# An im2col kernel on one core: four equal stores of two channels, and copies of several planes in one instruction

## The chip, the cores and the metric

The kernel runs on one core of a Trainium2 chip. The metric is the time of one execution on the device in microseconds (us), as a median of several executions. The profile shows one execution by itself; its span, from the first to the last instruction, is about 1.8 us shorter than the time.

"Engine" stands for two things here. VectorE and ScalarE copy data, and SyncE issues the transfers. The transfers themselves are carried by sixteen DMA engines: the page gives the time of the queue's packets as a share of sixteen engines' span, and packets start in rounds of sixteen (in the kernel before, 786 GB/s times 0.50 us are sixteen rows of 24,576 bytes). The views used here do not name a packet's engine. That each engine goes on with its own next packet is read from the times: in the kernel before, the sixteen last load packets end between 11.20 and 11.63 us, and the store's first sixteen packets start at just those times, one for one within 0.02 us. A packet is mostly one row, the bytes of one partition: 24,576 in the second load, 32,400 in a store of one channel, 64,800 in a store of two (112 of the 1008 packets of the kernel before are under 512 bytes). A transfer is *issued* when SyncE hands it to the queue, and has *landed* when its completion is seen.

## The reference

The operation is called im2col (image to columns). The input `x` is 16 images of 64 channels of 32 x 32 float32. For each channel and each of the nine positions (ki, kj) of a 3 x 3 window, the output holds one *plane*: the 30 x 30 elements of the channel that start at (ki, kj).

```python
for i in range(h_out):            # 30
    for j in range(w_out):        # 30
        patch = x[b, :, i:i + kernel_size, j:j + kernel_size].copy()
        cols[b, :, col_idx] = patch.ravel()
        col_idx += 1
```

Nothing is computed. 4.19 MB are read and 33.18 MB are written.

## The kernel before

The 1024 (image, channel) pairs are laid out as 128 partitions of 8 channels. Two loads bring them in: channels 0 and 1 first, then the other six. VectorE and ScalarE copy planes, 900 elements at a time, into an output tile of two channels, of which there are two buffers, and SyncE stores the tile. Channels 0 and 1 are stored separately; the other three pairs have one store each. All transfers go through one DMA queue.

```python
out_pool = ctx.enter_context(tc.tile_pool(name="out_pool", bufs=2))
# ... (cut)
first = load(nc.sync, 0, 2 * H)
load(nc.sync, 2 * H, CPP * H)

on_act = (False, True, False, True, False)
n = 0
for c in range(0, CPP, 2):
    out_tile = out_pool.tile([P, 2, KK, HO, WO], x.dtype, name="out_tile")
    for s in range(2):
        for kk in range(KK):
            ki, kj = divmod(kk, K)
            src = in_tile[:, c + s, ki : ki + HO, kj : kj + WO]
            dst = out_tile[:, s, kk]
            if kk % 3 != 1 if c + s == 0 else on_act[n % len(on_act)]:
                nc.scalar.copy(out=dst, in_=src)
            else:
                nc.vector.tensor_copy(out=dst, in_=src)
            n += 1
        if c == 0:
            nc.sync.dma_start(out=out_v[:, s], ...)           # one channel, arguments cut
    if c > 0:
        nc.sync.dma_start(out=out_v[:, c : c + 2] ..., ...)   # two channels, arguments cut
```

## Time and profile before

| | before |
|---|---|
| time, median of 3 runs | 91.28 us (91.22 to 91.31) |
| span in the profile | 89.5 us |
| VectorE, ScalarE busy | 25%, 31% |
| queue's packets, of sixteen engines' span | 97.2% |
| first store issued | 9.92 us |
| last store issued, landed | 56.64 us, 88.7 us |

The row to start from is the queue's 97.2%: the copying engines idle for most of the span, the transfers hardly ever do.

(A line of a timeline gives start and duration in us, the engine, the line of the kernel, the operation, output<-input and the count; SPq is SyncE issuing transfers.)

### The profile page before, as it was taken

The page shows a single profiled execution, that of the slowest core. Times are in us where ns is not written, and L with a number is a line of the kernel's source. Part 1 is how long each engine was busy: PE and PEld are TensorE (multiplying, and loading weights), DVE is VectorE, ACT ScalarE, POOL GpSimd, SP SyncE. Part 2 cuts the span into 40 slices and gives each one's busy share as a digit, 9 for nine tenths or more (in the row PEclk, how much of TensorE's full clock was granted, in tenths as well). Part 3 has the DMA queues.
Part 4 walks back from the last instruction along what each step waited for, and adds up shares of the span by engine and source line. Part 5 has one row for each costly group of instructions (what it writes and reads, how often), then busy time and mean ns, then how long its engine had stood idle before and what let it go on. Part 6 is the DMA issues. An engine that isn't in the chain of part 4 may idle for free.

```text
span 89.5 us, 136 instructions
## 1 busy us (share of the span) xinstructions
DVE 22.4 (25%) x41; ACT 27.7 (31%) x32; POOL 0.2 (0%) x4
## 2 busy tenths in 40 slices
DVE  0089369900000099400000499200000000000000
ACT  5089999910000099900000499200000000000000
POOL 0000000000000000000000000000000000000000
DMA  5989899999989999996699999999999996779990
GB/s 146 498 373 505 351 463 463 463 463 434 405 376 405 695 463 463 463 405 290 290 405 463 463 463 463 463 463 463 463 463 463 463 463 290 318 318 463 463 463 0
DMA packets 1008, 37.37 MB, mean 417 GB/s; under 512 B 112, under 2 KB 112, under 8 KB 112
## 3 DMA queue, kind: packets, MB, share of 16 engines
q1 hardware_dynamic: 1008, 37.37, 97.2%
HBM read 4.19 MB, written 33.18 MB: 417 GB/s over the span
## 4 chain that ended last, share of the span: by engine, by line
DMA 41%; ACT 15%; DVE 6%; DVEq 1%; issue 0%
DMA out_dram<-out_tile 36%; ACT out_tile L54 15%; DVE out_tile L56 6%; DMA in_tile<-in_x_dram 5%; DVEq L82 1%; DVEq L56 0%
## 5 line engine op out<-in xcount | busy, mean ns | idle before, releaser
L54 ACT COPY out_tile<-in_tile 128x900 f32<-128x900 f32 x31 | 26.5, 938 | 28.0 <-DMA out_dram<-out_tile 25.4
L56 DVE COPY out_tile<-in_tile 128x900 f32<-128x900 f32 x41 | 22.4, 624 | 34.2 <-DMA out_dram<-out_tile 27.1
L54 ACT ACT_TABLE_LOAD x1 | 1.3, 1283 | 0.8 <-PEq L111 0.8
L111 POOL MEMSET const-bfloat16-1.0<- 128x1 bf16 x1 | 0.1, 102 | 0.0
L111 POOL MEMSET const-uint8-127<- 128x1 uint8 x1 | 0.1, 102 | 0.0
L111 POOL MEMSET const-float32-1.0<- 128x1 f32 x1 | 0.1, 99 | 0.0
L111 POOL MEMSET const-float32-0.0<- 128x1 f32 x1 | 0.1, 98 | 0.2 <-issue 0.2
## 6 DMA issues: line engine op xcount, KB each, us to landing
out_dram<-out_tile SPq DMA_DIRECT2D x3, 8100.0 KB, 32.1
out_dram<-out_tile SPq DMA_DIRECT2D x2, 4050.0 KB, 15.3
in_tile<-in_x_dram SPq DMA_DIRECT2D x1, 3072.0 KB, 11.2
in_tile<-in_x_dram SPq DMA_DIRECT2D x1, 1024.0 KB, 4.7
```

Of the source, the lines that this page charges most:

```text
L54: nc.scalar.copy(out=dst, in_=src)
L56: nc.vector.tensor_copy(out=dst, in_=src)
L82: tc.compile()
L111: nc = _bacc.Bacc("TRN2", target_bir_lowering=False, num_devices=1)
```

## The change

The intent is to have fewer and larger instructions and transfers. Planes of one row of the window start one element apart, so one instruction can copy two or three of them if the source pattern gets an additional outermost dimension of step 1. VectorE takes two planes (`kj` 0 and 1) at a time, ScalarE three. In the first channel of each pair VectorE also takes the planes (0, 2) and (2, 2) in one instruction, which start two rows apart; in the second channel these two are copied singly, one by each engine. Channels 0 and 1 are no longer stored apart: there are four equal stores.

```diff
+    def planes(c, ki, kj, n, step):
+        w = in_tile[:, c, ki : ki + HO, kj : kj + WO]
+        part, row, col = [list(d) for d in w.ap]
+        return bass.AP(w.tensor, w.offset, [part, [step, n], row, col])
 ... (cut: the loop over kk, its choice of engine, and the stores of one channel go)
         for s in range(2):
+            o = out_tile[:, s]
+            nc.scalar.copy(out=o[:, K : 2 * K], in_=planes(c + s, 1, 0, K, 1))
+            for ki in (0, 2):
+                nc.vector.tensor_copy(
+                    out=o[:, ki * K : ki * K + 2], in_=planes(c + s, ki, 0, 2, 1)
+                )
+            if s == 0:
+                nc.vector.tensor_copy(
+                    out=o[:, 2:KK:6], in_=planes(c + s, 0, 2, 2, 2 * W)
+                )
+            else:
+                nc.vector.tensor_copy(out=o[:, 2], ...)       # one plane, arguments cut
+                nc.scalar.copy(out=o[:, 8], ...)              # one plane, arguments cut
+        nc.sync.dma_start(out=out_v[:, c : c + 2] ..., ...)   # for every c
```

More of the change, by code (lines that the diff above doesn't have):

```diff
@@ L19, in _im2col @@
     CPP = B * C // P
-    assert CPP * P == B * C and C % CPP == 0 and CPP % 4 == 0
+    assert CPP * P == B * C and C % CPP == 0 and CPP % 2 == 0 and K == 3
     x_v = x.rearrange("b (cp c2) h w -> (b cp) (c2 h w)", c2=CPP)
@@ L31, in _im2col, with load @@
     in_flat = in_tile.rearrange("p c h w -> p (c h w)")
-    def load(queue, r0, r1):
-        return queue.dma_start(
-            out=in_flat[:, r0 * W : r1 * W], in_=x_v[:, r0 * W : r1 * W]
-        )
-    first = load(nc.sync, 0, 2 * H)
-    load(nc.sync, 2 * H, CPP * H)
-    on_act = (False, True, False, True, False)
-    n = 0
+    def load(r0, r1):
+        return nc.sync.dma_start(
+            out=in_flat[:, r0 * W : r1 * W],
+            in_=x_v[:, r0 * W : r1 * W],
+        )
+    first = load(0, 2 * H)
+    load(2 * H, CPP * H)
+    def planes(c, ki, kj, n, step):
+        w = in_tile[:, c, ki : ki + HO, kj : kj + WO]
+        part, row, col = [list(d) for d in w.ap]
+        return bass.AP(w.tensor, w.offset, [part, [step, n], row, col])
     for c in range(0, CPP, 2):
@@ L48, in _im2col @@
         for s in range(2):
-            for kk in range(KK):
-                ki, kj = divmod(kk, K)
-                src = in_tile[:, c + s, ki : ki + HO, kj : kj + WO]
-                dst = out_tile[:, s, kk]
-                if kk % 3 != 1 if c + s == 0 else on_act[n % len(on_act)]:
-                    nc.scalar.copy(out=dst, in_=src)
-                else:
-                    nc.vector.tensor_copy(out=dst, in_=src)
-                n += 1
-            if c == 0:
-                nc.sync.dma_start(
-                    out=out_v[:, s],
-                    in_=out_tile[:, s].rearrange("p kk i j -> p (kk i j)"),
-                )
-        if c > 0:
-            nc.sync.dma_start(
-                out=out_v[:, c : c + 2].rearrange("p c n -> p (c n)"),
-                in_=out_tile.rearrange("p c kk i j -> p (c kk i j)"),
-            )
+            o = out_tile[:, s]
[3 more added lines that the diff above has]
+                    out=o[:, ki * K : ki * K + 2], in_=planes(c + s, ki, 0, 2, 1)
+                )
+            if s == 0:
[3 more added lines that the diff above has]
+            else:
+                nc.vector.tensor_copy(
+                    out=o[:, 2], in_=in_tile[:, c + s, 0:HO, 2 : 2 + WO]
+                )
+                nc.scalar.copy(
+                    out=o[:, 8], in_=in_tile[:, c + s, 2 : 2 + HO, 2 : 2 + WO]
+                )
+        nc.sync.dma_start(
+            out=out_v[:, c : c + 2].rearrange("p c n -> p (c n)"),
+            in_=out_tile.rearrange("p c kk i j -> p (c kk i j)"),
+        )
     return first
```

## The prediction

> **What bounds the kernel now.** I began with the page of the profile. VectorE and ScalarE are busy a quarter and a third of the span; the DMA engines are nearly always busy.
>
> ```profile
> span 89.5 us, 136 instructions
> DVE 22.4 (25%) x41; ACT 27.7 (31%) x32; POOL 0.2 (0%) x4
> q1 hardware_dynamic: 1008, 37.37, 97.2%
> ```
>
> The reader is to see that one DMA queue moves 37.37 MB, and that the time of its packets fills 97.2% of what sixteen engines have. Those bytes (4.19 MB in, 33.18 MB out) are fixed by the task, and the change touches none of them. So what matters is whether the queue ever runs dry. I read the timeline next: when each engine copies, and when each transfer is issued.
>
> ```profile
> 4.74 13.60 ACT L54 COPY out_tile<-in_tile 128x900 f32<-128x900 f32 x16 [2.67 <-DMA in_tile<-in_x_dram]
> 4.74 4.93 DVE L56 COPY out_tile<-in_tile 128x900 f32<-128x900 f32 x9 [4.74 <-DMA in_tile<-in_x_dram]
> 9.92 2.87 SPq L59 DMA_DIRECT2D out_dram<-out_tile  x2
> 12.02 6.00 DVE L56 COPY out_tile<-in_tile 128x900 f32<-128x900 f32 x11 [2.35 <-DMA in_tile<-in_x_dram]
> ...
> 50.56 6.00 DVE L56 COPY out_tile<-in_tile 128x900 f32<-128x900 f32 x11 [13.66 <-DMA out_dram<-out_tile]
> 56.64 0.33 SPq L64 DMA_DIRECT2D out_dram<-out_tile  x1
> ```
>
> The first load lands at 4.7 us, the second at 12.0. The store of channel 0 is issued at 9.92, before the second load has landed. The last store is issued at 56.64 and lands 32.1 us later (DMA issues of the page), at 88.7: it stood in the queue behind others for most of that time. To find gaps in the queue I asked for the table of windows in narrow stretches. Its last two columns are DMA share and GB/s, and a packet is counted in the window in which it starts, so a share can be over 1 and a window without a start shows 0.
>
> ```profile
> 0.00:1.00 1.00, 0.00 (x0) 0.21 (x1) 0.20 (x4) 1.00 0.00 0
> 1.00:1.45 0.45, 0.00 (x0) 0.45 (x1) 0.00 (x0) 1.00 1.43 291
> 10.25:10.75 0.50, 0.00 (x0) 0.50 (x2) 0.00 (x0) 1.00 1.82 786
> 10.75:11.20 0.45, 0.00 (x0) 0.45 (x1) 0.00 (x0) 1.00 0.00 0
> 11.20:11.65 0.45, 0.00 (x0) 0.45 (x2) 0.00 (x0) 1.00 2.69 1152
> 12.35:12.85 0.50, 0.50 (x2) 0.50 (x2) 0.00 (x0) 1.00 2.40 1037
> ...
> 30.35:30.80 0.45, 0.00 (x0) 0.00 (x0) 0.00 (x0) 1.00 5.34 2304
> 32.75:33.20 0.45, 0.45 (x2) 0.45 (x2) 0.00 (x0) 1.00 5.32 2304
> 85.40:85.85 0.45, 0.00 (x0) 0.00 (x0) 0.00 (x0) 1.00 5.33 2304
> ```
>
> Three things are to be seen. First, the sixteen engines start their packets together, spread over about 0.43 us: 786 GB/s times 0.50 us is 393 KB, sixteen rows of 24,576 bytes, the last of the second load; 1152 times 0.45 is 518 KB, sixteen rows of 32,400 bytes, the first of the store. Second, the share gives a packet's time: 1.82 times 0.50 us is 0.91 us. The load's last packets start from about 10.29, so they end from about 11.20, just where the store's first ones start: **no gap**. Third, the rows of the large stores (2304 times 0.45 is 1037 KB, sixteen of 64,800 bytes) take 5.33 times 0.45 = 2.40 us each. From 30.35 to 85.40 lie 55.05 us, which is 23 of them at 2.39. From 11.2 us to the end the queue never waits for the copies: the store of the third buffer is issued at 38.28 and starts at about 49.5, so that compute is over 11 us early.
>
> [...] 16 times 64,800 bytes in 2.39 us is 434 GB/s. [...]
> [...] Here the first load is issued at 0.00 and its first packet starts in the window from 1.00 us on; steps of 0.02 us inside it put the start at about 1.03, and I use this measured value.
> [...] eleven VectorE copies take 6.00 us and one takes 624 ns, so one starts every (6.00 - 0.624)/10 = 538 ns[...]. ScalarE: (13.60 - 0.938)/15 = 844 ns[...].
> [...]
>
> **The change, part by part.**
> (1) Copies are merged. VectorE goes from 41 instructions to 24, ScalarE from 31 copies to 12. One pair of channels costs VectorE five copies of two planes and one of one plane: [...], plus about 0.09 until the last one ends (624 - 538), 5.66. ScalarE has two copies of three planes and one of one: [...], plus 0.09 (938 - 844), 5.63. Before, a pair took 6.00. So 0.34 us is saved for each pair, but for the second, third and fourth pair this lies wholly beside stores that take 19 us each: worth 0.
> (2) The first store is now of two channels, not one. Compute starts at 4.74 as before; the store may be issued at 4.74 + 5.66 + 0.02 = **10.42** in place of 9.92: 0.50 later, although it waits for twice the planes. This is where the merging is needed: at the old cost per plane the 18 planes would have been ready at 4.74 + 6.00 = 10.74.
> (3) What does 0.50 us cost? The engines are free for the store from 11.20. With 1.03 us from issue to first packet, the store starts at 10.42 + 1.03 = 11.45, so the queue would stand still for **0.25 us**. Everything behind it is one chain of packets, so this goes to the end undiminished.
> (4) One transfer less, and no rows of 32,400 bytes: channels 0 and 1 took from 11.20 to 30.39 = 19.19 us as two stores; as one store they should take 8 rows of 2.39 = 19.1. **-0.08 us**.
> (5) The second pair's store is issued at 12.02 + 5.66 = 17.7, while the first store runs to about 30.6: hidden. The third waits for the first store to land (31.4 before, about 31.6 now), takes 5.7 us and is issued at about 37.3, needed at about 49.6. The tail, one landing after the last packet, is unchanged.
> Sum: +0.25 - 0.08 = +0.17 us; 91.28 becomes about 91.45, and I round up to **91.5**, since the errors lie more on the late side.
>
> **The rivals.**
> [...] Each paired source is two planes one element apart[...]. For it: nothing in this trace shows such a copy[...]. [...] I give it 8%.
> *The start latency is shorter for a store than I took.* [...] In the kernel before, the store was issued 1.28 us before its first packet, so its own latency is only known to be no longer than that. If it were 1.28, the gap would be 0.5 us and the time 91.7.
> *Fewer instructions and transfers make it faster.* This is the intent. Against it: 86 us of packets[...] plus 1.0 us ahead of the first and about 1.3 after the last are already the whole span but for about a microsecond. Over 2% would need 1.8 us; there is nowhere to take it from. 1%.
>
> **Range and chances.** The gap's uncertainty is 0 to 0.5 us, run to run spread is 0.09 us, and a partly slowed VectorE pulls upward: 91.1 to 92.1 for eight in ten. Faster 0.01, same 0.91, slower 0.08.
>
> **What would show it.** VectorE two-plane copies of about 1.09 us[...] and ScalarE three-plane copies of about 2.44; the first store issued near 10.4; in narrow windows, first packets of 64,800 bytes (2304 over 0.45 us) starting near 11.45 and none before; then a row every 2.39 us to the end, with the last store landing about 0.2 us later than 88.7. [...] a wait by the queue in the middle of the kernel would refute my reading that the later pairs are hidden.

Passages that state or use rules and figures that no trace or run of this case shows are cut from it; the cuts are marked. +0.25 us for the gap and -0.08 us for the transfer less come to +0.17 us, so 91.28 becomes 91.45, rounded up to 91.5. But terms behind the gap are cut. It rests on 5.66 us for the copies of a pair (5.63 on ScalarE), of which only the last 0.09 us has its working left. The rest, like the 1.09 and 2.44 us expected of a single copy, was estimate, from copy rates that the trace of before does not show. The trace of the changed kernel shows the 5.66 us itself (from 4.93 to 10.59), and copies of 1.09 and 2.44 us.

Three more things were assumed there and not shown. That no copies make the queue faster: the trace shows that sixteen rows of 64,800 bytes take 2.39 us, and 37.37 MB at that rate, 434 GB/s, are the 86 us of packets in the third rival. That the gap could be as small as 0: it stands as estimate. And the first rival, of which little but its chance of 8% is left: that VectorE copies two planes one element apart in one instruction more slowly than estimated.

## More of the kernel before

All runs quoted here were with a granted clock of 1.0.

The page's chain of work that ended last is easily misread here. In the kernel before it is

```profile
DMA 41%; ACT 15%; DVE 6%; DVEq 1%; issue 0%
```

It follows waits of engines, so it gives ScalarE 15% for copies of the first 18 us, beside which the queue was busy with the loads. Whether those copies cost anything is told by the gaps between packets, not by this line; the prediction looks for them in narrow windows.

## The result, and the profile after

The changed kernel took **91.25 us** (median of 6 runs, 91.10 to 91.39); the kernel before, in 6 runs, 91.30. The ratio is 0.9992, with a 95% interval of 0.9977 to 1.0007: the same time. Ratios, here and below, are the mean time of one kernel's fast runs over that of the other's in the same rounds, so they are not quite the ratios of the medians quoted.

First the page of the profile of the changed kernel: totals, its chain of work that ended last, the queue, and the groups of copies (busy us, mean ns of one, idle time before them).

```profile
span 89.6 us, 96 instructions
DVE 22.6 (25%) x24; ACT 23.8 (27%) x13; POOL 0.2 (0%) x4
...
q1 hardware_dynamic: 864, 37.37, 97.2%
...
DMA 49%; DVE 12%; DVEq 1%; issue 0%; SPq 0%
...
L55 ACT COPY out_tile<-in_tile 128x2700 f32<-128x2700 f32 x8 | 19.2, 2443 | 31.7 <-DMA out_dram<-out_tile 27.1
L57 DVE COPY out_tile<-in_tile 128x1800 f32<-128x1800 f32 x16 | 16.8, 1092 | 33.7 <-DMA out_dram<-out_tile 27.1
L61 DVE COPY out_tile<-in_tile 128x1800 f32<-128x1800 f32 x4 | 4.4, 1090 | 0.0
```

ScalarE's busy time fell by 3.9 us, there are 40 instructions fewer, and the queue's share stayed at 97.2%. The chain's first stretch is now VectorE's and no longer ScalarE's; the time is the same. A two-plane copy takes 1.09 us. The timeline of the changed kernel shows the end of the first pair's copies and the issue of the first store:

```profile
4.93 4.79 ACT L55 COPY out_tile<-in_tile 128x2700 f32<-128x2700 f32 x2 [2.87 <-DMA in_tile<-in_x_dram]
...
9.97 0.62 DVE L65 COPY out_tile<-in_tile 128x900 f32<-128x900 f32 x1
10.69 46.03 SPq L71 DMA_DIRECT2D out_dram<-out_tile  x4
```

In this execution the first load landed 0.2 us later than in the profile of before (4.9 against 4.7), and the second load 0.2 us later with it (12.2 against 12.0). Such shifts appear from execution to execution with one and the same kernel (4.93 here, 4.70 in the changed kernel's other profile, `after_again`; 4.6 to 5.0 over all the runs below), so the issue has to be read against the end of the load in the same trace. The narrow windows of the changed kernel (last columns: DMA share and GB/s, a packet counted where it starts) show the turn from load to store:

```profile
10.30:10.34 0.04, 0.04 (x1) 0.04 (x1) 0.00 (x0) 1.00 1.43 614
10.90:10.93 0.03, 0.00 (x0) 0.00 (x0) 0.00 (x0) 1.00 1.90 819
10.95:11.50 0.55, 0.00 (x0) 0.00 (x0) 0.00 (x0) 1.00 0.01 0
11.50:11.85 0.35, 0.00 (x0) 0.00 (x0) 0.00 (x0) 1.00 6.94 2962
11.52:11.54 0.02, 0.00 (x0) 0.00 (x0) 0.00 (x0) 1.00 7.62 3240
11.82:11.84 0.02, 0.00 (x0) 0.00 (x0) 0.00 (x0) 1.00 7.50 3240
```

The first DMA engine starts its last load packet at about 10.33 us and the last one at about 10.92, each of 0.91 us. So the engines come free between **11.24 and 11.83**. All sixteen start the store between **11.54 and 11.84**. The first engine stood still for 0.3 us, the last one not at all. From the issue at 10.69 to the first packet it is 0.85 us.

### The profile page after: what moved, and what is told of

It reads as the page before. It is cut to its first block, busy times and chain, and to the rows that moved or that the text cites. A ratio compares the mean times of both kernels' runs of the same rounds, so it can differ in the third digit from the quotient of the medians.

```text
span 89.6 us, 96 instructions
## 1 busy us (share of the span) xinstructions
DVE 22.6 (25%) x24; ACT 23.8 (27%) x13; POOL 0.2 (0%) x4
## 2 busy tenths in 40 slices
DMA packets 864, 37.37 MB, mean 417 GB/s; under 512 B 96, under 2 KB 96, under 8 KB 96
## 3 DMA queue, kind: packets, MB, share of 16 engines
q1 hardware_dynamic: 864, 37.37, 97.2%
## 4 chain that ended last, share of the span: by engine, by line
DMA 49%; DVE 12%; DVEq 1%; issue 0%; SPq 0%
DMA out_dram<-out_tile 36%; DMA in_tile<-in_x_dram 13%; DVE out_tile L57 8%; DVE out_tile L61 2%; DVE out_tile L65 1%; DVEq L89 1%; DVEq L57 0%; SPq L71 0%
## 5 line engine op out<-in xcount | busy, mean ns | idle before, releaser
L55 ACT COPY out_tile<-in_tile 128x2700 f32<-128x2700 f32 x8 | 19.2, 2443 | 31.7 <-DMA out_dram<-out_tile 27.1
L57 DVE COPY out_tile<-in_tile 128x1800 f32<-128x1800 f32 x16 | 16.8, 1092 | 33.7 <-DMA out_dram<-out_tile 27.1
L61 DVE COPY out_tile<-in_tile 128x1800 f32<-128x1800 f32 x4 | 4.4, 1090 | 0.0
L68 ACT COPY out_tile<-in_tile 128x900 f32<-128x900 f32 x4 | 3.8, 938 | 0.0
L65 DVE COPY out_tile<-in_tile 128x900 f32<-128x900 f32 x4 | 2.5, 620 | 0.0
## 6 DMA issues: line engine op xcount, KB each, us to landing
in_tile<-in_x_dram SPq DMA_DIRECT2D x1, 3072.0 KB, 11.4
```

The source lines that it names most:

```text
L55: nc.scalar.copy(out=o[:, K : 2 * K], in_=planes(c + s, 1, 0, K, 1))
L57: nc.vector.tensor_copy(out=o[:, ki * K : ki * K + 2], in_=planes(c + s, ki, 0, 2, 1))
L61: nc.vector.tensor_copy(out=o[:, 2:KK:6], in_=planes(c + s, 0, 2, 2, 2 * W))
L65: nc.vector.tensor_copy(out=o[:, 2], in_=in_tile[:, c + s, 0:HO, 2 : 2 + WO])
L68: nc.scalar.copy(out=o[:, 8], in_=in_tile[:, c + s, 2 : 2 + HO, 2 : 2 + WO])
```

## The experiments

Each was run beside the kernel before on one chip. "Scratch copy" is a VectorE copy of one plane into a tile that nobody reads; its only use is to take 0.54 us (one starts every 0.54 us: eight took 4.39 us in `delay8`, one by itself 0.62 in `delay1`). All results were correct.

**1. The changed kernel again, and its two parts alone.** `merge_only` has the new copies with the stores of before; `stores_only` has the four equal stores with copies of one plane.

```diff
# merge_only, against the changed kernel
+            if c == 0:
+                nc.sync.dma_start(out=out_v[:, s], ...)     # one channel
+        if c > 0:
             nc.sync.dma_start(out=out_v[:, c : c + 2] ..., ...)
# stores_only, against the kernel before
-                if kk % 3 != 1 if c + s == 0 else on_act[n % len(on_act)]:
+                if on_act[n % len(on_act)]:
-            if c == 0:
-                nc.sync.dma_start(out=out_v[:, s], ...)     # one channel
-        if c > 0:
         nc.sync.dma_start(out=out_v[:, c : c + 2] ..., ...)
```

> The changed kernel once more, beside the kernel before on this chip. Theory (the queue is the bound, and the first store reaches the slowest DMA engine just as it comes free): 91.2 to 91.3 us, ratio 0.998 to 1.001. Rival (the predicted gap of 0.25 us is real and was hidden by noise): ratio about 1.002.

> Four equal stores with the one-plane copies of before. Theory: the first pair takes 6.00 us instead of 5.66, so the first store is issued at about 11.0 us, 0.35 us later than in the changed kernel, which has no spare time there: 91.5 to 91.6 us, ratio about 1.003. Rival (the stores themselves bring a gain, the copies do not matter): the same as the changed kernel, 91.25 us.

> The merged copies with the stores of before (channel 0 and 1 stored apart). Theory: the first store is issued near 8.1 us, the second near 10.7, both before the loads have drained, so there is no gap, and the time is that of the kernel before, 91.3 us, ratio 0.999 to 1.001. Rival (fewer instructions are worth something): 0.5 us or more faster.

The changed kernel again took 91.15 us, ratio 0.9981 (0.9968 to 0.9994); `stores_only` 91.36 us, ratio 1.0005 (0.9991 to 1.0019). The first is what the theory said. The second lies between the two: 0.22 us above the changed kernel, where the theory had about 0.3 and the rival nothing; experiment 2 says why. `merge_only` took **92.68 us, ratio 1.0145** (1.0126 to 1.0164). Neither the theory nor its rival had that: one part of the change, by itself, makes the kernel slower by 1.3 us. Its timeline shows the first store's issue, and its narrow windows the end of the second load:

```profile
7.97 0.35 SPq L72 DMA_DIRECT2D out_dram<-out_tile  x1
```

```profile
8.45:8.95 0.50, 0.50 (x2) 0.50 (x1) 0.00 (x0) 1.00 1.84 786
9.40:9.90 0.50, 0.50 (x2) 0.50 (x2) 0.00 (x0) 1.00 2.98 786
10.45:11.45 1.00, 0.00 (x0) 0.00 (x0) 0.00 (x0) 1.00 1.59 393
12.00:13.10 1.10, 0.00 (x0) 0.00 (x0) 0.00 (x0) 1.00 1.10 471
```

Every line has sixteen packets; share times width is the mean time of one. The load packets of the first line take 0.92 us, those of the second 1.49 and the last ones of the load 1.59, against 0.91 for the same packets in the kernel before. The store's first packets (518 KB, the last line) start 0.8 to 1.4 us later than there. So the queue was never empty, but it ran slowly for two packets, after the first store had been put into it at 7.97 us. The merged copies alone are not the reason, for the changed kernel has the same ones and its last load packets take 0.91 us. Experiment 4 takes this up.

**2. How late may the first store be?** One, two, four and eight scratch copies ahead of the first store.

```diff
             o = out_tile[:, s]
+            if c + s == 1:
+                for n in range(8):          # 1, 2, 4 or 8
+                    nc.vector.tensor_copy(out=pad[:, n % 8], in_=in_tile[:, c, 0:HO, 0:WO])
```

> One VectorE copy of a plane into a scratch tile ahead of the first store: issue 0.54 us later, near 11.2 us. Theory (a late first store is paid in full, from a knee that the changed kernel stands on): 91.25 + 0.54 = 91.8 us, ratio about 1.005. Rival (the spread of the sixteen engines, 0.3 to 0.6 us, absorbs part of it): 91.3 to 91.5 us.

> Two scratch copies ahead of the first store: issue 1.08 us later, near 11.8 us. Theory (paid in full from the knee on): 91.25 + 1.08 = 92.3 us, ratio 1.011. Rival (spread of the engines absorbs up to 0.5 us): 91.8 us.

> Four such scratch copies ahead of the first store: issue 2.15 us later, near 12.85 us, first packet near 13.7. Theory (paid in full): 91.25 + 2.15 = 93.4 us, ratio 1.023. Rival (the queue makes up for a late start in the middle, where buffers wait for landings): clearly under 93 us.

> Eight scratch copies ahead of the first store: issue 4.3 us later. Theory: 91.25 + 4.3 = 95.55 us, ratio 1.047, and twice the effect of four. [...] Rival: the second doubling costs less than the first.

In `delay2` the store is issued at 11.61 us, when the load is practically over, and its narrow windows show how an idle queue starts:

```profile
10.95:12.40 1.45, 0.90 (x3) 0.33 (x1) 0.00 (x0) 1.00 0.01 0
12.40:12.65 0.25, 0.25 (x1) 0.25 (x1) 0.00 (x0) 1.00 9.72 4147
```

The sixteen packets start between 12.45 and 12.60: the first 0.85 us after the issue, the last 0.15 us after the first. So the last DMA engine starts about 1.00 us after the issue, and an estimate of the cost of a late store is *issue + 1.00 - the time at which the slowest engine has finished the load*, if that is positive. The issue and the end of the load are from the trace of each run itself, the 1.00 from `delay2`; the measured column is the difference of the ratios to that of the undelayed kernel (0.9981), times 91.4 us.

| run | time | ratio | issue | load finished, slowest engine | estimated cost | measured |
|---|---|---|---|---|---|---|
| after_again | 91.15 | 0.9981 | 10.45 | 11.56 | 0 (-0.11) | 0 |
| stores_only | 91.36 | 1.0005 | 10.76 | 11.54 | 0.22 | 0.22 |
| delay1 | 91.65 | 1.0027 | 10.86 | 11.48 | 0.38 | 0.42 |
| delay2 | 92.20 | 1.0085 | 11.61 | 11.64 | 0.97 | 0.95 |
| triple_on_vector (see 5) | 92.79 | 1.0151 | 12.14 | 11.55 | 1.59 | 1.55 |
| delay4 | 93.20 | 1.0197 | 12.54 | 11.53 | 2.01 | 1.97 |
| delay8 | 95.45 | 1.0436 | 14.90 | 11.76 | 4.14 | 4.16 |

The agreement is within 0.05 us. That is closer than the runs could promise, since each ratio is only known to 0.12 to 0.14 us either way, and `delay2` is no test of the 1.00 that it gave. A late first store is paid in full, and the queue gives nothing back later; but the spread of the engines at the end of the load leaves a margin, which the changed kernel uses up to within 0.1 us. `stores_only` fits the same line, so the merged copies are worth 0.2 us in this kernel, and all of it is gained before the first store. `delay1` lies between its theory (0.54) and its rival (0 to 0.25), since the margin takes up a part; the longer delays come out 0.1 to 0.2 us under their theory, as they should with that margin.

**3. How late may the third store be?** The same scratch copies, 8 or 24, ahead of the third store.

```diff
             o = out_tile[:, s]
+            if c + s == 5:
+                for n in range(8):          # 8 or 24
+                    nc.vector.tensor_copy(out=pad[:, n % 8], in_=in_tile[:, c, 0:HO, 0:WO])
```

> The same eight scratch copies, but ahead of the third store, where the queue holds work until about 49.9 us and the store is issued near 37.3 us. Theory: 4.3 us of the 11.8 us of slack are used and nothing is seen: 91.25 us, ratio 0.998 to 1.001. Rival (compute in the middle matters too, through buffers and their landings): up to 4.3 us slower.

> Twenty-four scratch copies ahead of the third store; [...] some 14.7 us in all. Theory: the slack of the third store is 49.9 - 0.85 - 37.3 = 11.8 us, so the rest shows: 2.5 to 3.5 us slower, 93.7 to 94.7 us. Rival (the middle is never on the path): 91.25 us.

`late8` took 91.25 us, ratio 0.9981 (0.9968 to 0.9993): the same as the undelayed kernel's. 4.3 us of additional copies cost nothing. `late24` took 92.70 us, ratio 1.0141 (1.0127 to 1.0155). Its scratch copies took 13.0 us in all, 0.54 us each, not the 14.7 expected (that the last sixteen would take longer was an estimate that no trace showed), so the time lies under the expected 93.7 to 94.7 us, and the store was issued at 50.00 us:

```profile
50.00 0.33 SPq L79 DMA_DIRECT2D out_dram<-out_tile  x1
```

```profile
47.30:47.55 0.25, 0.25 (x2) 0.00 (x0) 0.00 (x0) 1.00 9.58 4147
47.55:50.80 3.25, 2.71 (x4) 0.33 (x1) 0.00 (x0) 1.00 0.00 0
50.80:51.00 0.20, 0.20 (x1) 0.20 (x1) 0.00 (x0) 1.00 12.14 5184
```

The timeline gives the issue, the windows the rows of the second store that end near 49.90 us on the slowest DMA engine (start 47.50, 2.40 each), and the first rows of the third between 50.83 and 50.98. The gap is 1.08 us, and the estimate of experiment 2 gives 50.00 + 1.00 - 49.90 = 1.10. The third store has its slack of over 11 us, and work ahead of it costs nothing until that is used up. Against `late8` the time rose by 1.45 us, 0.4 us more than the gap; all four executions of this run took 2.2 us more than their spans (the profiled one 92.69 against 90.5), where those of the other runs took about 1.8 more, so those 0.4 us lie outside the span. Why is open.

**4. Why was the early store slow?** Two theories for `merge_only`: the first store was queued too early behind the load (E), or the second store, queued at 10.5 us behind the first, did it (S). `early_then_late` keeps the early first store and delays the second by four scratch copies. `split_late` was meant to issue two stores of one channel late.

```diff
# early_then_late, against merge_only
             o = out_tile[:, s]
+            if c + s == 1:
+                for n in range(4):
+                    nc.vector.tensor_copy(out=pad[:, n % 8], in_=in_tile[:, c, 0:HO, 0:WO])
# split_late, against the changed kernel
+        if c == 0:
+            for s in range(2):
+                nc.sync.dma_start(out=out_v[:, s], ...)     # after both channels' copies
+        else:
             nc.sync.dma_start(out=out_v[:, c : c + 2] ..., ...)
```

> As merge_only, with four scratch copies ahead of the second store: the first store is issued near 8.0 us as there, the second near 12.7, after the loads have drained. merge_only cost 1.3 us because the last two packets of the second load took 1.56 us instead of 0.91. Theory E (a store queued so early, 3.6 us ahead of the end of the load, slows the load): slow again, 92.6 us, ratio 1.014. Theory S (the second store, issued at 10.5 us while the load and the first store were still queued, slows it): as the kernel before, 91.3 us, ratio 1.000.

> The changed kernel with its first store split into the two channels, both issued after the pair is complete, near 10.45 and 10.8 us, so that two stores are queued behind the load as in merge_only, but the first not early. Theory E: no slow load packets, 91.3 us, ratio 0.999 to 1.001. Theory S: slow load packets, up to 1.3 us more. If neither this run nor the other is slow, both conditions are needed together.

`early_then_late` took 92.61 us, ratio 1.0135 (1.0114 to 1.0156): slow as E has it. Its timeline has the first store at 7.96 us and the second 4.7 us later, near 12.6; its narrow windows have the last two rounds of load packets:

```profile
7.96 5.03 SPq L80 DMA_DIRECT2D out_dram<-out_tile  x2
```

```profile
9.40:9.90 0.50, 0.50 (x2) 0.50 (x2) 0.00 (x0) 1.00 2.60 786
10.70:11.40 0.70, 0.70 (x2) 0.00 (x0) 0.00 (x0) 1.00 2.33 562
```

That is 1.30 and 1.63 us a packet, and all of these packets had started by 11.4 us, while only one store was queued. **S falls.** `split_late` was a bad test: 92.52 us, ratio 1.0120, but it was not what I meant to build. The first store waited for the copies of its own channel and not for its place in the program: it was again issued early, at 8.22 us, while the copies of the second channel ran until 10.68:

```profile
8.22 2.88 SPq L73 DMA_DIRECT2D out_dram<-out_tile  x2
```

The last two rounds of its load packets are slow too, 1.10 and 1.50 us each:

```profile
9.40:10.15 0.75, 0.75 (x2) 0.75 (x2) 0.00 (x0) 1.00 1.46 524
10.50:11.15 0.65, 0.18 (x1) 0.15 (x1) 0.00 (x0) 1.00 2.31 605
```

It says nothing of S, and it is hardly a third kernel: each engine is given the same instructions in the same order as in `merge_only`, so it is that kernel run again on another chip. What the three runs share, and no other has, is a store issued at 8.0 to 8.2 us, with three rounds of load packets (of 0.91 us) still to start. In the kernel before the store is issued at 9.92 us, with one round to start, and that round takes its 0.91 us. So the association is shown in two kernels. All three runs also combine merged copies with stores of one channel, and no run has that combination with a late first store (`split_late` was to be it), nor an early store with the old copies; so it isn't shown that the early issue alone is enough. Where the threshold lies, and what in the DMA engines does it, is open too: no run varied the early issue in small steps.

**5. The choice of two planes for VectorE and three for ScalarE.** In `triple_on_vector` the groups change engines.

```diff
-            nc.scalar.copy(out=o[:, K : 2 * K], in_=planes(c + s, 1, 0, K, 1))
+            nc.vector.tensor_copy(out=o[:, K : 2 * K], in_=planes(c + s, 1, 0, K, 1))
             for ki in (0, 2):
-                nc.vector.tensor_copy(
+                nc.scalar.copy(
                     out=o[:, ki * K : ki * K + 2], in_=planes(c + s, ki, 0, 2, 1)
                 )
```

> The groups of three planes go to VectorE and the groups of two to ScalarE; nine planes of a pair on each engine. [...] ScalarE needs 4 x 1.594 + 0.844 + 0.094 = 7.3 us for a pair, so the first store is issued near 12.3 us, 1.65 later than in the changed kernel. Theory: 91.25 + 1.65 = 92.9 us, ratio 1.018; the second to fourth pair hide.

The 1.594 us for a copy of two planes on ScalarE was an estimate; the traces give about the same, midway between a start every 0.84 us with one plane (before) and every 2.35 us with three (the changed kernel, 4.79 - 2.44). In this run four of them took 6.48 us.

It took 92.79 us, ratio 1.0151 (1.0138 to 1.0165), with the first store at 12.14 us. The groups of its copies by shape:

```profile
L55 DVE COPY out_tile<-in_tile 128x2700 f32<-128x2700 f32 x8 | 23.7, 2962 | 30.0 <-DMA out_dram<-out_tile 25.3 <-DMA in_tile<-in_x_dram 4.7
L61 DVE COPY out_tile<-in_tile 128x1800 f32<-128x1800 f32 x4 | 4.4, 1088 | 0.0
...
L65 DVE COPY out_tile<-in_tile 128x900 f32<-128x900 f32 x4 | 2.5, 620 | 0.0
```

From one plane to two, 900 elements more take 468 ns, which is 0.52 ns an element and leaves 152 ns of the 620 over its elements, if the first plane goes at the same rate. The three-plane copy takes 2962 - 152 = 2810 ns for 2700 elements, 1.04 ns each if those 152 ns are the same: half the rate. So here three planes in one instruction took VectorE 2.96 us, against 1.09 us for two, and they are better left to ScalarE, which took 2.44 us in the changed kernel. Why is not shown, and no other number of planes was run.

## Why the prediction was right or wrong

The prediction was right: 91.25 us lies in its range of 91.1 to 92.1, the class was "same", and 91.5 was 0.25 us too high. The range was wide enough for a gap and for none, so that it held says little of part (3), the one term that was wrong. By its own steps:

- **The bound.** Right. The queue's share is 97.2% in both kernels, and `late8` shows directly that 4.3 us more work ahead of the third store is free.
- **Part (1), the copies.** The estimates were right in each number: 1.09 us for the two-plane copy and 2.44 for the three-plane one, as predicted; a pair takes 10.59 - 4.93 = 5.66 us, as predicted. The 0.34 us saved per pair counts only in the first, as `stores_only` shows (0.22 us, the rest is margin).
- **Part (2), the issue of the first store.** Predicted 10.42. Where the first load landed at 4.7 us as before (`after_again`) it was 10.45; in the profile shown above, 10.69, of which 0.2 us is the later landing. In both traces, where VectorE ends last, the issue follows 0.1 us after its end, not the 0.02 I took.
- **Part (3), the gap of 0.25 us.** This is the term that was mis-sized: for the end of the kernel it was 0. Two things were wrong in it. The first packet follows the issue of a store by 0.85 us (10.69 to 11.54 in the changed kernel, 11.61 to 12.46 in `delay2`); 1.03 was taken from the first load. With 0.85 the same sum would have given 0.07 us. And I compared the first free engine with the first packet, where the slowest DMA engine counts: it comes free 0.59 us after the first (11.83 against 11.24) and starts the store 0.30 us after the first (11.84 against 11.54). The first engine did stand still, for 0.3 us; the last engine, which ends the kernel, did not.
- **Part (4), -0.08 us.** Not shown. From the end of the load on the slowest engine to the end of the last row are 76.59 us before (11.63 to 88.22) and 76.49 after (11.83 to 88.33), but 76.60 in `late8`, which has the same four stores (11.58 to 88.18), and 76.54 in `merge_only` with five (13.08 to 89.61). The traces differ among themselves by as much as the term. The three comparisons with the kernel before (0.9992, 0.9981, and 0.9981 in `late8`, which differs only in hidden work) say -0.07 to -0.17 us; two of the three intervals leave out 1, but which term that comes from is open.
- **Part (5), later pairs hidden.** Right. The third store was expected to have over 11 us to spare: 8 scratch copies vanish, 24 overshoot by the gap worked out and by 0.4 us more, which stay open.
- **The rival of a slower copy of two planes** falls: with planes one element apart it takes 1092 ns, and 1090 with planes two rows apart, which is the 1.09 us expected. **The rival of a shorter start latency** was right that there is no gap, but only in part for its reason: the latency is 0.85 us rather than 1.03, which alone would leave 0.07 us of gap, and the slowest DMA engine does the rest. **Faster by fewer instructions** did not come about.

Where the expected gain of a change with 40 instructions and one transfer less went: most of the copies it shortens ran beside the stores. In front of the first store the merged copies earn 0.2 us over the old ones, and the larger first store needs just that to be in time.

## What to carry to other kernels

In a kernel whose transfer queue is full, look for the places where the queue could run dry, and compare at each the issue plus the measured start latency with the time at which the *slowest* DMA engine comes free; here a deficit there was paid in full (in `delay8` 4.16 us, where 4.14 were worked out). Copies that run beside a store of 19 us could here be made 0.34 us faster a pair, or 4.3 us slower, without effect, because their store had over 11 us to spare. And issuing a store earlier isn't automatically harmless: here, with merged copies and stores of one channel, a store put in the queue some 3.5 us ahead of the usual end of the load went with a load that ended 1.2 to 1.4 us later.
